# Gated delta net in a two-layer trunk: the decay block's product in front of the state's product, inverse copies of odd pairs on VectorE, and memsets moved ahead

## The chip, the core and the metric

The kernel runs on one core of one Trainium2 chip. The metric is device time in microseconds (us), the median of the runs of one kernel. Before the change it is 2989.25 us over three runs (2982.93 to 2990.8).

## What is computed

A trunk of two layers on a sequence of 1024 positions with 1024 features, all in float32. Layer 0 mixes with a gated delta net of 8 heads, layer 1 with a retention layer of 4 heads; behind each mixer stand a layer norm and a gated convolution feed-forward. The change touches only the delta net. Cut to what matters, with chunks of 64 in the reference:

```python
kk = strict_lower(einsum(kb, k) * decay)
sol = triangular_solve(kk + eye, [v * beta, kb * exp(gc)])
u, w = sol
qk = lower(einsum(q, k) * decay)
def step(state, inp):
    q_n, k_n, u_n, w_n, qk_n, g_n = inp
    v_new = u_n - w_n @ state
    o = (q_n * exp(g_n)) @ state + qk_n @ v_new
    state = state * exp(g_last) + (k_n * exp(g_last - g_n)).T @ v_new
    return state, o
```

Per head, the state of a chunk depends on that of the chunk before it. Everything else of the layer is matrix products that can be put anywhere between.

## The kernel before

**Work.** Here a chunk has 128 positions, so a head has 8 chunks (`NCH`). The delta net is written as Python generators: `gates`, `filler`, `t_path`, `t_decay`, `t_chain`, `prep`, `dt_half`, `scan`, `tail`, `load_q`. The function `run` decides at build time in which order they issue. It keeps a clock that advances by an assumed cost of each TensorE instruction, and always goes on with the ready generator of best priority. A generator that has issued something whose result it needs says how long that will take, by `yield LAT[...]`: only after that many microseconds of planned TensorE work may it go on. `LAT["s1"]`, `["s2"]` and `["s3"]` (1.9, 1.4 and 1.8) are these for the three legs of a scan step, `LAT["T0"]` that for the copies in `t_chain`. Generators also wait for named events (`after_ev`) and for free buffers (`take`, `give`). The order is then fixed on TensorE; every other engine has its instructions in the order in which they were written down, and works them off one after the other.

**The filler.** `filler` has the lowest priority. Its list `items` names projections of 128 features each: "c" (a convolved q, k or v projection that stays in SBUF), "s" (the same, stored to memory and loaded later by a second "c" entry or by `load_q`), "z" (the gate's projection). Each projection is 16 units of three 512-column products, `acc<-hT,wl` and two `acc<-hT,wh`; the units go into the places where nothing of higher priority is ready. Behind each "c" and "s" come a ScalarE copy and scale per half (L485, L488), three VectorE multiply-adds per half (L490) and a SiLU (L491).

**Heads.** Heads go in two groups of four ("quads"), in each quad two pairs: pair 0 and pair 2 are even, 1 and 3 odd. For a quad, `t_decay` makes the decay block of each head (`U`), `t_path` the k-k products and then a forward substitution on VectorE that inverts the four 32x32 diagonal blocks of every chunk; results are `RX` and `TX`. `t_chain` (per pair) copies these into `T0` (L926, three copies of 32x256 per head) and into the inverse's tile `R` (L937 on ScalarE for two row blocks, L939 on GpSimd for the other two, 32x128 each), after zeroing `R` on GpSimd (L931), and then completes the inverse by small products (`mm<-T,U`, `mm<-R,xa` and others). `prep` transposes and scales v and k (evictions L1003, L1012), `dt_half` makes the decay block of q and k, `DT` (L1032).

**The scan step.** `scan` runs per head; the four heads of a quad are in it together. Even pairs write to the PSUM banks named `sc`, odd pairs to those named `mm`, two banks each. In step n all products of a head go to four quarters of one bank: p1 = k times state, p4 = q times state, p2 = `R` times v (named `sc<-qkv,R`), p5 = `U` times w (the state's product, `sc<-w,U`), and p3 = `DT` times w (the decay block's product, `sc<-w,DT`), in the quarter of p1. VectorE makes the new v from p1 (L1059), ScalarE makes w from p2 (L1063) and scales p4 (L1065); VectorE makes the next state `Sn` from p5 (L1073; L1071 in step 0) and adds p3 to the output (L1081). Before the change the state's product and the instruction for `Sn` are issued first, then the decay block's product. All TensorE instructions are issued through helpers, so that they carry line L714 (products) or L717 (transposes); the tile's name tells them apart.

Of the kernel before, what the change touches and what calls it, by code (L numbers as in the profile page):

```python
# [9 lines left out]
F32 = mybir.dt.float32  # L10
# [23 lines left out]
def trunk_kernel(ctx: ExitStack, tc, A):  # L34
# [11 lines left out]
    def tl(tag, shape, dt=F32, name=None):  # L46
        return sb.tile(shape, dt, tag=tag, name=name or tag, bufs=BUFS[tag])

    def two(tag, dt=F32, name=None):
        if tag in ("qkv", "auh"):  # L50
            return tl(tag, [P, HALF], dt, name), tl(tag, [P, HALF], dt, name)
        t = tl(tag, [P, 2, HALF], dt, name)
        return t[:, 0], t[:, 1]
# [659 lines left out]
    def pm(out, lhsT, rhs, start=True, stop=True, cost=0.216):  # L713
        pq(pe.matmul(out, lhsT, rhs, start=start, stop=stop), cost)  # L714
# [4 lines left out]
    def after_ev(*names):  # L719
        return ("ev", names)  # L720

    def emit(name, lat=0.0):
        events[name] = clk[0] + lat
# [45 lines left out]
    def take(tag, n):  # L769
        while free[tag] < n:  # L770
            yield lambda: free[tag] >= n
        free[tag] -= n

    def give(tag, n):
        free[tag] += n
# [39 lines left out]
    dve.tensor_scalar(mneg, m_incl, 1e30, -1e30, ALU.mult, ALU.add)  # L815

    def decay(h):
        for q4 in range(2):
            yield from take("t2", 2)
            gm = [tl("t2", [P, 4, P], F32R, name="gm") for _ in range(2)]  # L820
            for t, g in zip(gm, (gh64, gl64)):
                pool.tensor_tensor(t, bm(m_incl, 4), bc(g[:, q4s(q4), h], P), ALU.mult)
            yield LAT["gm"]
            pt = acc_tile() if h > 3 else sc_tile()
            pm(pt, m_lowr, gm[1], start=True, stop=False)
            pm(pt, m_lowr, gm[0], start=False, stop=True)
            dve.tensor_tensor(U[h][:, q4s(q4)], v4(pt), bm(mneg, 4), ALU.add)
            give("t2", 2)

    def t_decay(p):  # L830
        yield after_ev(("g",), ("DD", p - 1), ("T", p // 2 - 1))
# [10 lines left out]
    def t_path(g):  # L842
        heads = quads[g]
        X = None
        if g:
            yield after_ev(*[("Sh", h) for h in quads[g - 1]])
        for hh, h in enumerate(heads):
            yield after_ev(("f", GH + h), ("DD", h // 2))
            sk = tl("sm", [P, NCH], name="sk")
            cj[h] = tl("sm", [P, NCH], name="cj")  # L850
            ir[h] = tl("sm", [P, NCH], name="ir")
            for q4 in range(2):
                yield LAT["kk"]
                pt = mm_tile()
                for c in range(4):
                    ks = fx(GH + h, q4 * 4 + c)
                    pm(pt[:, c * P:(c + 1) * P], ks, ks)
                for c in range(4):
                    n = q4 * 4 + c
                    junk = tl("S", [P, P], name="jk")  # L860
                    dve.scalar_tensor_tensor(junk, pt[:, c * P:(c + 1) * P], 1.0, ident, ALU.mult, ALU.mult,
                                             accum_out=sk[:, n:n + 1])
                qs = q4s(q4)
                dve.tensor_scalar(sk[:, qs], sk[:, qs], 1e-6, None, ALU.add)
                dve.reciprocal(cj[h][:, qs], sk[:, qs])
                dve.tensor_tensor(cj[h][:, qs], cj[h][:, qs], beta[:, qs, h], ALU.mult)
                if q4:
                    pool.tensor_tensor(ir[h], sk, phalf, ALU.pow)
                for c in range(4):
                    n = q4 * 4 + c  # L870
                    dve.scalar_tensor_tensor(U[h][:, n], pt[:, c * P:(c + 1) * P], cj[h][:, n:n + 1],
                                             U[h][:, n], ALU.mult, ALU.mult)
            if X is None:
                yield from take("lane", 1)
                X = tl("lane", [P, 32, 32], name="X")
            for b in range(4):
                bs = slice(32 * b, 32 * b + 32)
                act.activation(X[bs, :, hh * 8:hh * 8 + 8].rearrange("p i c -> p c i"), U[h][bs, :, bs], AF.Copy)
        yield from take("lane", 2)
        yield LAT["X"]  # L880
        Y = tl("lane", [P, 32, 32], name="Y")
        dve.transpose(flat(Y), flat(X))
        T = tl("lane", [P, 32, 32], name="T")
        pool.memset(T, 0.0)
        pool.memset(flat(T)[:, 0:1024:33], 1.0)
        tmp = tl("fs", [P, 256], name="fs")
        for j in range(31):
            ni, nj = 31 - j, j + 1
            tv = tmp[:, 0:ni * nj].rearrange("p (i j) -> p i j", j=nj)
            dve.tensor_tensor(tv, bc(Y[:, j + 1:, j], nj), bm(T[:, j, 0:nj], ni), ALU.mult)  # L890
            ts_ = T[:, j + 1:, 0:nj]
            dve.tensor_tensor(ts_, ts_, tv, ALU.subtract)
            if j % 3 == 2:
                yield LAT["fs"]
        RX = tl("lane", [P, 32, 32], name="RX")
        dve.transpose(flat(RX), flat(T))
        TP = tl("lane", [P, 32, 32], name="TP")
        act.activation(TP, T.rearrange("p i j -> p j i"), AF.Copy)
        TX = tl("lane", [P, 32, 32], name="TX")
        dve.transpose(flat(TX), flat(TP))  # L900
        RTX[g] = (RX, TX)
        give("lane", 1)
        emit(("T", g), LAT["T"])
# [4 lines left out]
    def dx_(h, n):  # L908
        return DT[h, n // 4][:, n % 4 * P:n % 4 * P + P]

    def t_chain(p):
        heads = pairs[p]
        yield after_ev(("T", p // 2))
        RX, TX = RTX[p // 2]
        cx = p % 2 * 16
        yield from take("auh", 4)
        yield from take("lane", 1)
        T0 = tl("lane", [P, 2, NCH, 64], name="T0")
        lo, hi = slice(0, 64), slice(64, 128)
        for hh, h in enumerate(heads):  # L920
            ch = slice(cx + hh * 8, cx + hh * 8 + 8)
            pool.memset(T0[0:32, hh, :, 32:64], 0.0)
            for b in range(3):
                bs = slice(32 * b, 32 * b + 32)
                cs = slice(32, 64) if b == 1 else slice(0, 32)
                act.activation(T0[bs, hh, :, cs], TX[bs, :, ch].rearrange("p i c -> p c i"), AF.Copy)  # L926
        for hh, h in enumerate(heads):
            R[h] = two("auh", F32, "R")
            for q4 in range(2):
                Rv = v4(R[h][q4])  # L930
                pool.memset(Rv, 0.0)  # L931
                ch = slice(cx + hh * 8 + q4 * 4, cx + hh * 8 + q4 * 4 + 4)
                for b in range(4):
                    bs = slice(32 * b, 32 * b + 32)
                    src = RX[bs, :, ch].rearrange("p i c -> p c i")
                    if b < 2:
                        act.activation(Rv[bs, :, bs], src, AF.Copy)  # L937
                    else:
                        pool.tensor_copy(Rv[bs, :, bs], src)  # L939
        if ("T0", p ^ 1) in events:  # L940
# [98 lines left out]
    def scan(p, h):  # L1039
# [9 lines left out]
        for n in range(NCH):  # L1049
# [14 lines left out]
            if n:  # L1064
                act.activation(vn, p4, AF.Copy, scale=egc[:, n, h:h + 1])  # L1065
            yield LAT["s2"]
            if n < NCH - 1:
                pm(p5, U[h][:, n], w)
                Sn = tl(home, [P, P], name="Sn")
                if n == 0:  # L1070
                    dve.tensor_copy(Sn, p5)  # L1071
                else:
                    dve.scalar_tensor_tensor(Sn, S0, egl[:, n, h:h + 1], p5, ALU.mult, ALU.add)  # L1073
                S0 = Sn
            if n % 4 == 0:
                yield after_ev(("D", h, n // 4))
            pm(p3, dx_(h, n), w)
            if n == 0:
                act.activation(vn, p3, AF.Copy)
            else:  # L1080
# [58 lines left out]
    def filler(items):  # L1139
        for kind, ti in items:  # L1140
# [44 lines left out]
            if kind != "z":  # L1185
# [5 lines left out]
                    emit(("f", ti), LAT["fv"])  # L1191
            bg_step(acc_tile)

    LAT = {"kk": 3.6, "exp": 3.2, "ld": 6.0, "g1": 12.0, "gm": 3.0, "mm": 2.2, "T": 6.0, "X": 3.4, "fs": 4.85, "T0": 5.5, "t1": 2.0, "t2": 3.3, "t3": 1.7, "D": 2.7, "s1": 1.9, "s2": 1.4, "s3": 1.8, "tail": 12.5, "ssq": 9.3, "fv": 4.0}
    events["T", -1] = events["DD", -1] = 0.0
    pairs = [(2 * p, 2 * p + 1) for p in range(GH // 2)]
    c, z = "c", "z"
# [1 line left out]
    s = "s"  # L1199
    quads = [tuple(range(4)), tuple(range(4, 8))]  # L1200
    items = [("h", 1), ("h", 2), ("h", 3), (c, K + 2), (c, K + 3), (z, 0), (c, V), (c, V + 1), (c, V + 2), (c, V + 3), (c, 1),
             (s, 2), (s, 3), (s, K + 4), (s, K + 5), (s, K + 6), (z, 1), (z, 2), (c, K + 4), (c, K + 5), (c, K + 6),
             (c, K + 7), (s, 6), (s, 7), (c, V + 4), (c, V + 5), (c, V + 6), (c, V + 7), (c, 4), (c, 5),
             (z, 3), (z, 4), (z, 5), (z, 6), (z, 7)]
    todo = [(-1.0, gates()), (9.0, filler(items)), (0.3, t_path(0)), (2.3, t_path(1)), (0.9, load_q(1)), (2.9, load_q(3))]
    for p in range(4):
        q = p & 2
# [889 lines left out]
```

## Time and profile before

| what | us |
|---|---|
| median of three runs | 2989.25 |
| the profiled execution's own time | 3002.74 |
| its span in the profile | 3000.6 |
| TensorE (PE) busy | 2835.7 (95%) |
| weight loads (PEld) busy | 2309.8 |
| VectorE (DVE) busy | 2180.1 (73%) |
| ScalarE (ACT) busy | 1310.3 |
| GpSimd (POOL) busy | 505.3 |

The profiled execution's time lies 0.45% above the median. The delta net's generators cover roughly 100 to 698 us of the span. PE is busy nearly everywhere, so time is read as the waits of PE and as the clock that it was granted: the row PEclk of the page and the clock column of the view by windows give that as a share of full speed. A busy time at clock 0.5 holds half the work. An entry "PE sc L714 <- DVE Sn L1073" in the view of waits reads: PE stood idle before a product into a bank `sc` until the VectorE instruction at line 1073 was done. A matmul of 128x128 float32 counts as two instructions in the trace (two passes).

### The profile page before, as it was taken

The numbers are of one execution on the slowest core, as the hardware profiler recorded it, in microseconds if no ns is written. First come the engines' busy times: TensorE is split into PE (matmuls) and PEld (weight loads), VectorE is DVE, ScalarE is ACT, GpSimd is POOL, SyncE is SP. The second block draws the span as 40 slices with busy tenths as digits, with TensorE's granted clock in tenths as the row PEclk, the third lists the DMA queues.
The fourth block names the chain that finished last, engine by engine and source line by source line (L and its number), as shares of the span: only waits on it lengthen the run. The fifth ranks groups of instructions, "written<-read, shape, count | busy, mean of one in ns | idle before, by whom it ended". The sixth has DMA issues, their size and how long they took to land. (4 is left out here: it accounts for less than half of the span.)

```text
span 3000.6 us, 38751 instructions
## 1 busy us (share of the span) xinstructions
PE 2835.7 (95%) x13594; PEld 2309.8 (77%) x13594; DVE 2180.1 (73%) x3846; ACT 1310.3 (44%) x2413; POOL 505.3 (17%) x509
## 2 busy tenths in 40 slices
PE   8998799979999999999999999999999999999997
PEld 6787678867777888887778777777777787888886
DVE  5795559547588888867776775566778787777779
ACT  4754345433454444553543333122335444444543
POOL 0311031100002333210000011422111022332201
PEclk9997999899999999999999999999999999999999
DMA  7222233236425565565543355665564154434853
GB/s 268 96 85 90 86 111 110 68 111 209 162 71 175 187 210 180 197 236 167 176 134 127 109 174 174 213 190 160 179 236 141 73 175 144 136 132 151 305 186 113
DMA packets 253460, 468.44 MB, mean 156 GB/s; under 512 B 24209, under 2 KB 77841, under 8 KB 253265
## 3 DMA queue, kind: packets, MB, share of 16 engines
q1 hardware_dynamic: 218272, 409.59, 41.5%
q10 hardware_dynamic: 32352, 47.72, 4.3%
q0 software_dynamic: 2640, 8.65, 0.8%
q8 instruction: 107, 1.75, 0.2%
q14 instruction: 89, 0.72, 0.1%
HBM read 348.43 MB, written 117.44 MB: 155 GB/s over the span
## 5 line engine op out<-in xcount | busy, mean ns | idle before, releaser
L714 PE MATMUL acc<-hT,wh 128*128 128x512 f32 x960 | 302.2, 396 | 0.0
L1559 PE MATMUL acc<-bb,ab 128*128 128x512 f32 x984 | 236.2, 398 | 13.3 <-DVE bb L90 11.6
L1559 PEld LDWEIGHTS acc<-bb,ab 128*128 128x128 f32 x984 | 186.3, 191 | 57.4 <-DVE bb L90 16.0
L1261 PE MATMUL acc<-T,wb 128*128 128x512 f32 x840 | 203.5, 391 | 8.5 <-DVE wb L90 8.4
L714 PEld LDWEIGHTS acc<-hT,wh 128*128 128x128 f32 x960 | 183.9, 192 | 34.9
L89 ACT ACTIVATE ab<-ar 128x512 fp32r<-128x512 f32 x210 | 130.3, 626 | 173.8 <-PE mm L303 48.8
L714 PE MATMUL acc<-hT,wl 128*128 128x512 f32 x480 | 201.0, 419 | 2.8 <-DVE wl L90 1.6
L411 POOL TENSOR_TENSOR xg<-xg,gb 128x512 f32<-128x512 f32 x48 | 63.5, 1325 | 780.8 <-DMA xg<-xs 476.2
L1261 PEld LDWEIGHTS acc<-T,wb 128*128 128x128 f32 x840 | 156.6, 188 | 45.9 <-DVE wb L90 11.6
L90 DVE TENSOR_TENSOR wl<-wr,wh 128x1024 fp32r<-128x1024 f32 x98 | 123.1, 1256 | 94.6 <-ACT wh L89 94.0
L90 DVE TENSOR_TENSOR ab<-ar,ab 128x512 fp32r<-128x512 f32 x210 | 147.2, 706 | 58.0 <-ACT ab L89 58.0
L1724 POOL TENSOR_TENSOR o<-o 128x512 f32<-128x512 f32 x80 | 137.4, 1727 | 283.6 <-DVE o L1716 138.8
L89 ACT ACTIVATE wh<-wr 128x1024 fp32r<-128x1024 f32 x98 | 103.7, 1059 | 164.6 <-PE acc L714 60.5
L90 DVE TENSOR_TENSOR wb<-wr,wb 128x512 fp32r<-128x512 f32 x162 | 117.9, 732 | 72.4 <-ACT wb L89 70.7
L90 DVE TENSOR_TENSOR wb<-mm,wb 128x512 fp32r<-128x512 f32 x216 | 145.7, 683 | 26.2 <-ACT wb L89 25.3
L89 ACT ACTIVATE wb<-mm 128x512 fp32r<-128x512 f32 x216 | 124.4, 596 | 79.5 <-DVE mm L1315 76.6
L1693 DVE SCALAR_TENSOR_TENSOR o<-g,vc,o 128x512 f32<-128x512 f32 (+2 forms) x176 | 153.8, 892 | 3.8 <-ACT o L1688 3.1
L89 ACT ACTIVATE wb<-wr 128x512 fp32r<-128x512 f32 x162 | 98.3, 627 | 104.8 <-DMA wr<-in_ffn_up 44.3
L1331 ACT ACTIVATE pc<-acc 128x512 f32<-128x512 f32 x143 | 84.7, 592 | 132.9 <-PE acc L1261 83.6
L714 PE MATMUL acc<-wh,hT 128*128 128x512 f32 x384 | 135.1, 415 | 1.0 <-DVE vv L90 1.0
L110 PE MATMUL acc<-T,wb 128*128 128x512 f32 x292 | 115.4, 395 | 5.7 <-DVE wb L90 5.7
L239 DVE SCALAR_TENSOR_TENSOR ada<-mvw,e,ada 128x512 f32<-128x512 f32 x140 | 105.0, 750 | 15.8 <-DMA mvw<-in_ada_w 15.4
(669 smaller groups left out, 7427.8 us busy)
## 6 DMA issues: line engine op xcount, KB each, us to landing
wr<-in_ffn_up SPq DMA_DIRECT2D x92, 512.0 KB, 4.2
mvw<-in_ada_w SPq DMA_DIRECT2D x80, 512.0 KB, 4.6
ad<-o SPq DMA_DIRECT2D x154, 256.0 KB, 3.0
ar<-ad SPq DMA_DIRECT2D x154, 256.0 KB, 3.9
Br<-in_ffn_down SPq DMA_DIRECT2D x88, 256.0 KB, 3.5
wr<-in_ret_wv SPq DMA_DIRECT2D x32, 512.0 KB, 4.1
ar<-od SPq DMA_DIRECT2D x56, 256.0 KB, 5.2
wr<-in_gdn_wqkv SPq DMA_DIRECT2D x24, 512.0 KB, 3.5
```

The source lines that it names most:

```text
L89: act.activation(dst_h, src, AF.Copy)
L90: eng.tensor_tensor(dst_l, src, dst_h, ALU.subtract)
L110: mm(acc, wl[:, k], hl[0], start=first, stop=False)
L239: dve.scalar_tensor_tensor(a, wr[:, kk], e[:, k:k + 1], a, ALU.mult, ALU.add)
L411: pool.tensor_tensor(x, x, gb[0], ALU.mult)
L714: pq(pe.matmul(out, lhsT, rhs, start=start, stop=stop), cost)
L1261: return pe.matmul(*a, skip_group_check=True, **kw)
L1331: act.activation(t, X, AF.Copy)
L1559: return pe.matmul(*args, skip_group_check=True, **kw)
L1693: dve.scalar_tensor_tensor(tv, gv[:, c0 - j:c1 - j], w[:, 2 - j:3 - j], tv, ALU.mult, ALU.add)
L1724: (dve if fp == 0 else pool).tensor_tensor(o[d], o[x], o[y], op)
```

## The change

Five things change, all in the delta net:

- In a scan step the decay block's product (p3) is issued in front of the state's product (p5). The instruction for `Sn` still comes before the addition of p3 on VectorE.
- In `t_chain` of odd pairs the copies into `T0` and the first two row blocks of `R` are written for VectorE in place of ScalarE: per pair 6 copies of 32x256 and 8 of 32x128.
- `t_chain` takes the tiles of `R` and zeroes them when `t_path` reaches the event "X", ahead of the forward substitution, and no longer between the copies.
- `decay` of the heads of the second quad uses buffers of the tag "auh" in place of "t2". The odd scans hold all three "t2" buffers, so these decay blocks stood behind the scans of the first quad; now they can stand within them.
- The table: `LAT["T0"]` goes from 5.5 to 8.0, and in `items` the projection K+6 is no longer stored and loaded again but made once, in its later place, while z3 comes ahead.

```diff
     def decay(h):
+        home = "auh" if h > 3 else "t2"
         for q4 in range(2):
-            yield from take("t2", 2)
-            gm = [tl("t2", [P, 4, P], F32R, name="gm") for _ in range(2)]
+            yield from take(home, 2)
+            gm = [tl(home, [P, 4, P], F32R, name="gm") for _ in range(2)]
...
-            give("t2", 2)
+            give(home, 2)
...
         yield from take("lane", 2)
+        emit(("X", g))
         yield LAT["X"]
...
     def t_chain(p):
         heads = pairs[p]
+        yield after_ev(("X", p // 2))
+        yield from take("auh", 4)
+        for h in heads:
+            R[h] = two("auh", F32, "R")
+            for q4 in range(2):
+                pool.memset(R[h][q4], 0.0)
         yield after_ev(("T", p // 2))
         RX, TX = RTX[p // 2]
         cx = p % 2 * 16
-        yield from take("auh", 4)
         yield from take("lane", 1)
+
+        def block(out, src):
+            if p % 2:
+                dve.tensor_copy(out, src)
+            else:
+                act.activation(out, src, AF.Copy)
...
-                act.activation(T0[bs, hh, :, cs], TX[bs, :, ch].rearrange("p i c -> p c i"), AF.Copy)
+                block(T0[bs, hh, :, cs], TX[bs, :, ch].rearrange("p i c -> p c i"))
...
-                        act.activation(Rv[bs, :, bs], src, AF.Copy)
+                        block(Rv[bs, :, bs], src)
...
             yield LAT["s2"]
+            if n % 4 == 0:
+                yield after_ev(("D", h, n // 4))
+            pm(p3, dx_(h, n), w)
             if n < NCH - 1:
                 pm(p5, U[h][:, n], w)
                 Sn = tl(home, [P, P], name="Sn")
...
-            if n % 4 == 0:
-                yield after_ev(("D", h, n // 4))
-            pm(p3, dx_(h, n), w)
...
-             (s, 2), (s, 3), (s, K + 4), (s, K + 5), (s, K + 6), (z, 1), (z, 2), (c, K + 4), (c, K + 5), (c, K + 6),
+             (s, 2), (s, 3), (s, K + 4), (s, K + 5), (z, 1), (z, 2), (z, 3), (c, K + 4), (c, K + 5), (c, K + 6),
...
-             (z, 3), (z, 4), (z, 5), (z, 6), (z, 7)]
+             (z, 4), (z, 5), (z, 6), (z, 7)]
```

**TensorE, second step of the first quad's scans.** Four heads in one step, two in banks `sc` and two in banks `mm`; the words in brackets are the engines whose semaphores the instruction waits for. Before:

```order
L714 MATMUL sc_2683<-w_2723,U_823 128x128 [waits Activation_49]
L714 MATMUL sc_2683<-w_2723,DT_2136 128x128 [waits DVE_49]
L714 MATMUL sc_2687<-w_2731,U_880 128x128 [waits Activation_49]
L714 MATMUL sc_2687<-w_2731,DT_2136 128x128 [waits DVE_49]
L714 MATMUL mm_2718<-w_2720,U_1005 128x128
L714 MATMUL mm_2718<-w_2720,DT_2139 128x128 [waits DVE_49]
L714 MATMUL mm_2726<-w_2728,U_1093 128x128
L714 MATMUL mm_2726<-w_2728,DT_2139 128x128 [waits DVE_49]
```

The same place with the change:

```order
L714 MATMUL sc_2715<-w_2734,DT_2136 128x128 [waits Activation_49]
L714 MATMUL sc_2715<-w_2734,U_823 128x128
L714 MATMUL sc_2719<-w_2742,DT_2136 128x128 [waits Activation_49]
L714 MATMUL sc_2719<-w_2742,U_880 128x128
L714 MATMUL mm_2729<-w_2731,DT_2139 128x128
L714 MATMUL mm_2729<-w_2731,U_1005 128x128
L714 MATMUL mm_2737<-w_2739,DT_2139 128x128
L714 MATMUL mm_2737<-w_2739,U_1093 128x128
L714 MATMUL acc_2771<-q_2490,qkv_916 128x128 [waits DMAHW5_49]
L714 MATMUL sc_2777<-Sn_2753,qkv_651 128x128 [waits DVE_49]
```

Every product with `DT` waited for VectorE; now it stands first and waits, if at all, for ScalarE, the product with `U` behind it waits for nothing, and the first product of the next step waits for VectorE.

**VectorE, behind the forward substitution of the first quad.** `RX` and `TX` are its transposed results, L1003 (with the change L1014) evicts the transposed v, L490 is the convolution of a filler projection. Before:

```order
L896 STREAM_TRANSPOSE RX<-T 128x1024
L490 SCALAR_TENSOR_TENSOR oq<-raw,vc,oq 128x512
L900 STREAM_TRANSPOSE TX<-TP 128x1024
L1003 TENSOR_TENSOR qkv<-acc,ir 128x512
L490 SCALAR_TENSOR_TENSOR oq<-raw,vc,oq 128x512
L1003 TENSOR_TENSOR qkv<-acc,ir 128x512 x3
L511 TENSOR_SCALAR ssq_2148<-ssq_2148 128x8
```

With the change:

```order
L898 STREAM_TRANSPOSE RX<-T 128x1024
L490 SCALAR_TENSOR_TENSOR oq<-raw,vc,oq 128x512
L902 STREAM_TRANSPOSE TX<-TP 128x1024
L928 COPY R<-RX 32x4x32 x8
L1014 TENSOR_TENSOR qkv<-acc,ir 128x512
L490 SCALAR_TENSOR_TENSOR oq<-raw,vc,oq 128x512
L928 COPY T_2111<-TX 32x8x32 x6
L1014 TENSOR_TENSOR qkv<-acc,ir 128x512 x2
L511 TENSOR_SCALAR ssq_2148<-ssq_2148 128x8
```

Eight copies now stand in front of the first eviction of v and six more in front of the second.

**ScalarE at the same place.** `sq` (L509) are squares for a norm, four from each of two PSUM banks, `xa` belongs to the small products. Before:

```order
L898 ACTIVATE TP<-T 128x1024
L937 ACTIVATE R<-RX 32x4x32 x16
L509 ACTIVATE sq,ssq_2148<-acc 128x128 x3
L926 ACTIVATE T_2070<-TX 32x8x32 x6
L491 ACTIVATE oq<-oq 128x512
L926 ACTIVATE T_2103<-TX 32x8x32 x6
L509 ACTIVATE sq,ssq_2148<-acc 128x128 x4
```

With the change:

```order
L900 ACTIVATE TP<-T 128x1024
L930 ACTIVATE R<-RX 32x4x32 x8
L509 ACTIVATE sq,ssq_2148<-acc 128x128 x7
L930 ACTIVATE T_2086<-TX 32x8x32 x6
L509 ACTIVATE sq,ssq_2148<-acc 128x128
L491 ACTIVATE oq<-oq 128x512
```

The fourth square, which empties the first of the two banks, stood behind 28 copies and now stands behind 8.

More of the change, by code (lines that the diff above doesn't have):

```diff
@@ L925, in t_chain @@
                 cs = slice(32, 64) if b == 1 else slice(0, 32)
-                act.activation(T0[bs, hh, :, cs], TX[bs, :, ch].rearrange("p i c -> p c i"), AF.Copy)
+                block(T0[bs, hh, :, cs], TX[bs, :, ch].rearrange("p i c -> p c i"))
         for hh, h in enumerate(heads):
-            R[h] = two("auh", F32, "R")
             for q4 in range(2):
                 Rv = v4(R[h][q4])
-                pool.memset(Rv, 0.0)
                 ch = slice(cx + hh * 8 + q4 * 4, cx + hh * 8 + q4 * 4 + 4)
@@ L1192, in filler @@
             bg_step(acc_tile)
-    LAT = {"kk": 3.6, "exp": 3.2, "ld": 6.0, "g1": 12.0, "gm": 3.0, "mm": 2.2, "T": 6.0, "X": 3.4, "fs": 4.85, "T0": 5.5, "t1": 2.0, "t2": 3.3, "t3": 1.7, "D": 2.7, "s1": 1.9, "s2": 1.4, "s3": 1.8, "tail": 12.5, "ssq": 9.3, "fv": 4.0}
+    LAT = {"kk": 3.6, "exp": 3.2, "ld": 6.0, "g1": 12.0, "gm": 3.0, "mm": 2.2, "T": 6.0, "X": 3.4, "fs": 4.85, "T0": 8.0, "t1": 2.0, "t2": 3.3, "t3": 1.7, "D": 2.7, "s1": 1.9, "s2": 1.4, "s3": 1.8, "tail": 12.5, "ssq": 9.3, "fv": 4.0}
     events["T", -1] = events["DD", -1] = 0.0
```

## The prediction

> **What bounds the kernel now.** The page comes first: PE is busy for 95% of the span, and its clock is 0.9 or better in 40 coarse slices. Next come windows cut at the stages of the delta net, because an average over 3000 us hides them. The columns are the stretch, its length, busy time and count of each engine, granted clock, DMA share and GB/s.
>
> ```profile
> PE 2835.7 (95%) x13594; PEld 2309.8 (77%) x13594; DVE 2180.1 (73%) x3846; ACT 1310.3 (44%) x2413; POOL 505.3 (17%) x509
> 100.00:234.00 134.00, 128.14 (x608) 105.86 (x607) 111.06 (x284) 80.12 (x164) 28.03 (x37) 1.00 0.31 99
> 234.00:298.00 64.00, 50.95 (x613) 45.35 (x613) 31.57 (x62) 29.21 (x63) 8.40 (x24) 0.76 0.24 78
> 298.00:400.00 102.00, 82.56 (x477) 70.46 (x476) 49.68 (x125) 35.96 (x96) 12.29 (x16) 0.93 0.26 86
> 400.00:536.00 136.00, 130.43 (x621) 108.37 (x620) 111.43 (x285) 75.92 (x162) 30.53 (x41) 0.99 0.34 111
> 536.00:594.00 58.00, 56.35 (x651) 49.81 (x649) 26.83 (x55) 29.39 (x69) 7.71 (x20) 0.85 0.21 72
> 594.00:698.00 104.00, 80.26 (x482) 68.50 (x482) 52.48 (x137) 37.19 (x94) 8.41 (x8) 0.93 0.32 108
> ```
>
> The two scans (298 to 400, 594 to 698) leave PE idle for 19.4 and 23.7 us and run at clock 0.93; the stages of the forward substitution (100 to 234, 400 to 536) are nearly full. At 234 to 298, the inverse's chain of the first quad, there is a hole of 13 us and a clock of 0.76. VectorE has 50 of 102 us in a scan, so no engine is full there: what ends PE's idle time must be a wait. The waits of PE, first scan and then second, name it (total us, times, longest):
>
> ```profile
> PE sc L714 <- DVE Sn L1073: 9.2, 12, 1.8
> PE mm L714 <- DVE Sn L1073: 5.8, 10, 1.0
> PE sc L714 <- DVE qkv L1059: 2.9, 1, 2.9
> PE mm L714 <- DVE Sn L1071: 0.8, 2, 0.4
> PE sc L714 <- DVE Sn L1071: 0.8, 2, 0.4
> ...
> PE mm L714 <- DVE Sn L1073: 12.1, 12, 4.8
> PE sc L714 <- DVE Sn L1073: 6.5, 12, 1.3
> PE acc L717 <- DVE qkv L1101: 2.2, 2, 1.9
> PE mm L714 <- ACT qkv L1065: 1.4, 2, 1.3
> PE mm L714 <- DVE Sn L1071: 0.8, 2, 0.4
> PE sc L714 <- DVE Sn L1071: 0.8, 2, 0.4
> ```
>
> Almost all of it is one wait: for `Sn`, 16.6 us in the first scan and 20.2 in the second, 54 times. The timeline of one such place (start, length, engine, instruction, count, idle time before it) shows which product stands there.
>
> ```profile
> 602.03 0.30 PEld L714 LDWEIGHTS sc<-w,U 128*128 128x128 f32 x2
> 602.14 0.39 PE L714 MATMUL sc<-w,U 128*128 128x128 f32 x2
> 602.57 0.35 DVE L1073 SCALAR_TENSOR_TENSOR Sn<-Sn,eg,sc 128x128 f32<-128x128 f32 x1
> 602.97 0.30 PEld L714 LDWEIGHTS sc<-w,DT 128*128 128x128 f32 x2 [0.63 <-DVE Sn L1073]
> 602.97 0.49 PE L714 MATMUL sc<-w,DT 128*128 128x128 f32 x2 [0.44 <-DVE Sn L1073]
> 603.18 0.30 PEld L714 LDWEIGHTS sc<-w,U 128*128 128x128 f32 x2
> ```
>
> The product with `DT` does not read `Sn`. It waits because VectorE reads the state's product out of the same bank. The next product's weights are loaded 0.21 us behind its own (603.18 against 602.97), so without the wait it would have started 0.21 us after 602.14; it started 0.83 us after. That is 0.62 us lost, where the waits show 0.44: the end of a pipelined product is modelled late by about 0.18 us.
>
> **The scans: the wait that goes.** The first term is 36.8 us of waits for `Sn` plus 54 times 0.18, which is 9.7: **46 us** of TensorE time. With the decay block's product first, no read of the bank stands between the two products. It needs only w, as the state's product did before it. What is late next is the first product of the following step, which needs `Sn`; `Sn` itself comes 0.21 us later, since its product is second. From the start of the state's product to the end of `Sn` the rows above give 0.78 us, and the planner leaves 1.8 us of other work there, so the plain round trip is covered, by the other heads' products and filler units.
>
> **The scans: waits that come.** Bounds: nothing, if the planned times always suffice, and 46 us and more, if every wait moves to the next product. Of the 36.8 us, 54 times 0.44 are the plain round trip, 23.8; the other 13 are places where VectorE was late because of work ahead in its queue (longest 4.8 us). That lateness stays; I let half of it, 6 us, come back in front of products that read `Sn` or v. The product with `DT` now takes the wait for w on ScalarE. One step shows its size:
>
> ```profile
> 600.36 0.60 PE L714 MATMUL sc<-qkv,R 128*128 128x128 f32 x4
> 600.78 0.37 ACT L1063 ACTIVATE w<-sc,cj 128x128 f32<-128x128 f32 x1 [4.44 <-PE sc L714]
> 601.04 0.36 ACT L1065 ACTIVATE qkv<-sc,eg 128x128 f32<-128x128 f32 x1
> 601.29 0.37 ACT L1063 ACTIVATE w<-sc,cj 128x128 f32<-128x128 f32 x1
> ```
>
> w is done 0.79 us after its product starts, 1.30 with a second head's in front; the planner leaves 1.4 behind the product, so it fits narrowly: 4 us for the times when it doesn't. Together **10 us come back**, the value between the bounds that lies near the lower one, because the single row of a product waiting for anything but `Sn` in mid-scan is the one of 2.9 us.
>
> **The clock.** The scans hold 82.6 and 80.3 us busy at 0.93, which full speed would do in 5.8 and 5.6 us less. The stage from 100 to 234 us, 96% busy, has 1.00. Bounds 0 and 11; I take three quarters, as three quarters of the waits go: **8 us**.
>
> The clock of pieces of the first scan speaks for that: 0.83 and 0.91, where the waits' longest single entries were 1.8 and 2.9 us.
>
> ```profile
> 320.00:340.00 20.00, 16.11 (x85) 14.01 (x85) 10.94 (x31) 5.24 (x13) 3.26 (x5) 0.83 0.19 66
> 340.00:360.00 20.00, 15.78 (x93) 13.52 (x92) 12.51 (x33) 8.56 (x29) 3.44 (x4) 0.91 0.17 52
> ```
>
> The Trainium skill, "TensorE: Matmul & The Clock Gate" (section "HAM oscillation — how this bites in real kernels"), says that what costs the clock is a gap of more than about 3.4 us. By that rule short waits would cost no clock, this term would be 0, and the sum 8 us smaller. The rows disagree: the clock was low with no gap that long in the first scan.
>
> **The inverse's chain.** At 240 to 256 us TensorE waits for a bank that ScalarE empties:
>
> ```profile
> 236.49 2.58 ACT L937 ACTIVATE R<-RX 32x128 f32<-32x128 f32 x6 [0.33 <-DVE RX L896]
> 238.16 0.65 DVE L1003 TENSOR_TENSOR qkv<-acc,ir 128x512 f32<-128x512 f32 x1
> 238.87 0.33 PE L717 MATMUL acc<-cst,qkv 128*128 128x128 f32 x1 [2.21 <-DVE qkv L1003]
> ...
> 253.14 1.11 PE L717 MATMUL acc<-cst,qkv 128*128 128x128 f32 x4 [10.05 <-ACT sq L509]
> ...
> L926 ACT ACTIVATE T<-TX 32x256 f32<-32x256 f32 x12 | 7.5, 627 | 0.1
> L937 ACT ACTIVATE R<-RX 32x128 f32<-32x128 f32 x16 | 6.8, 425 | 0.5 <-DVE RX L896 0.3
> ```
>
> The fourth square stood behind 16 copies of 0.425 and 12 of 0.627. Now it stands behind 8 of the former: from 236.49 that is 239.9, and with four squares about 241. But 14 copies go to VectorE, in front of evictions of v. This trace has no copy from SBUF to SBUF on VectorE; the nearest rows are of the same shapes out of PSUM:
>
> ```profile
> L971 DVE TENSOR_SCALAR R<-mm 32x128 f32<-32x128 f32 x32 | 7.8, 279 | 0.3
> L967 DVE TENSOR_SCALAR T<-mm 32x256 f32<-32x256 f32 x8 | 3.3, 418 | 5.4 <-PE mm L714 5.3
> L490 DVE SCALAR_TENSOR_TENSOR qkv<-raw,vc,qkv 128x512 f32<-128x512 f32 x87 | 69.9, 803 | 17.4 <-ACT qkv L488 13.9 <-POOL gm L822 2.7 <-POOL ir L868 0.2
> ```
>
> 8 times 0.28 and 6 times 0.42 are 4.8 us, and the next evictions end about 246 in place of 242. TensorE goes on at about 246 to 247 where it went on at 253.1: **6 us gained** (bounds 0 and 11). In the second quad there was no hole (1.65 us idle in the whole chain), and the same copies now delay evictions that were on time: **4 us lost** (bounds 0 and 7). Net 2 us. The memsets are GpSimd's, whose 505 us leave room; they cost nothing.
>
> **The gap between the scans.** The second quad's decay blocks move into the first scan, on GpSimd and TensorE, the same number of instructions. K+6 and more convolutions fall into 400 to 536: by the new list 9 to 10 where there were 7, each six L490, 4.8 us of VectorE; some 12 us more on an engine with 25 us idle there. The stage at 100 to 234 has nine convolutions, and its PE idles no more than that at 400 (6 against 6 us). I charge **3 us**, bounds 0 and 12. The store and reload of K+6 go, hidden DMA either way.
>
> **The end of the second scan.** Two waits there, 2.2 and 1.4 us, come from a planner with nothing left to issue. With the change 12 filler units (three products each) stand behind and between the last steps: **3 us** gained.
>
> **Sum.** −46 + 10 − 8 − 2 − 3 + 3 = −46 us. Against the profiled execution's own 3002.7 that is 2957; it lies 13.5 us above the median, so against the median of 2989 the forecast is **2943 us**. Its own range, with waits that come between 0 and 25, the clock between 11 and 0 and the chain as bounded, is 2920 to 2965.
>
> **Rivals.** *Half of the wait comes back.* The scan legs are planned so tightly that without the accidental pauses VectorE and ScalarE are late by a few tenths at each of some 160 dependent products. For it: 13 us of lateness now. Against: no such wait but one in mid-scan. 23 us in place of 10 come back, and the clock gives 4 in place of 8: −29, **2960**; worse, with 35, 2972.
>
> *VectorE takes back the chain.* Its copies and GpSimd's copies (0.41 us each by the row below) keep each other out: 14 waits of 0.41 per quad, 11.5 us in all, behind which stand the evictions. Against it: the eviction and the convolution beside GpSimd's run (238.16, 0.65; the mean of L490 is 0.80) are not lengthened. **2955**, and 2964 with the whole 12 of the gap.
>
> ```profile
> L939 POOL COPY R<-RX 32x128 f32<-32x128 f32 x32 | 13.4, 418 | 1.5
> ```
>
> The Trainium skill, "SBUF — State Buffer" (section "Who interferes with whom"), names this: VectorE in a two-port mode and GpSimd lock each other out for whole instructions. By that rule the copies would cost what this rival says; no run here shows such a copy yet.
>
> *Slower: the recurrence is the bound.* If less than 1.04 us (0.83 + 0.21) of other work stands between the two products of a head and its next step's first, the whole wait moves there, and each is 0.21 us longer because `Sn` starts later: 54 times 0.21, 11 us, less 2 for the other terms: **2999**. Against it: three other heads' products and 1.8 us planned.
>
> *It does not do what it says*: the second product waits for something at the bank as the first did, and only the small terms remain: **2987**. The order shows no such wait.
>
> **How the numbers follow.** Forecast 0.60, half back 0.18, VectorE 0.09, no change 0.07, slower 0.06. A measurement of this kernel tells about 0.3% from no change, 9 us, so faster means under 2980: the first three, 0.87. The range takes in the forecast's bounds and the first two rivals, 2915 to 2975, and leaves out the last two.
>
> **What would show it.** Right: no wait "`DT` for `Sn`" in the waits; scans of some 80 us; clock near 1.00 in them; the 10 us wait for `sq` gone. Wrong: waits for `Sn` of like sum in front of `sc<-Sn,qkv`, waits for w above 10 us, or PE holes over 8 us at both chains.

## The result and the profile after

The changed kernel takes 2918.7 us (median of four runs, 2916.51 to 2920.75) against 2990.03 (four runs, 2982.93 to 2991.6): a ratio of 0.9766, with a 95% interval of 0.9748 to 0.9783, or 71 us less. Run again later beside other kernels it took 2919.27. The forecast was 46 us less: the sign and the main step were right, the size was 25 us too small.

The profiled execution after took 2919.49 us, 0.8 above its median; that of before took 3002.74, 12.7 above its own. So the two traces differ by 83 us where the kernels differ by 71, and some 10 us of the traces' difference lie where the change does next to nothing (4.5 ahead of the delta net's `RX`, 5.3 behind its end). First the page's row of engines and the windows of the changed kernel, cut at the same stages as in the prediction (stretch, length, busy time and count of PE, PEld, DVE, ACT and POOL, granted clock, DMA share, GB/s):

```profile
PE 2799.6 (96%) x13594; PEld 2288.3 (78%) x13594; DVE 2183.0 (75%) x3874; ACT 1299.3 (45%) x2387; POOL 494.8 (17%) x509
100.00:229.50 129.50, 123.66 (x589) 102.20 (x588) 106.77 (x280) 76.04 (x160) 24.34 (x35) 1.00 0.31 99
229.50:288.00 58.50, 52.15 (x620) 46.04 (x619) 37.93 (x76) 21.86 (x49) 8.68 (x23) 0.82 0.26 86
288.00:358.00 70.00, 68.71 (x470) 61.77 (x470) 46.49 (x125) 35.83 (x95) 21.44 (x20) 1.00 0.36 117
358.00:477.00 119.00, 117.18 (x565) 97.67 (x564) 100.35 (x274) 71.08 (x141) 20.39 (x38) 1.00 0.37 120
477.00:538.00 61.00, 54.11 (x654) 47.60 (x653) 39.10 (x81) 27.81 (x78) 9.39 (x21) 0.89 0.16 53
538.00:611.00 73.00, 71.61 (x485) 64.51 (x484) 46.95 (x130) 33.35 (x86) 7.43 (x7) 1.00 0.40 137
```

The scans (288 to 358, 538 to 611) took 206 us before and take 143. PE's idle time in them fell from 43.2 us to 2.7, and the clock rose from 0.93 to 1.00. PE's busy time fell by 22.5 us, though these windows hold about the same work: 959 instructions before and 955 now, of them 251 and 260 products of filler units. So the 22.5 us are the clock and the late modelled ends, and nearly all of the 63 us are gained in the scans. The stage from 358 to 477 stands for the earlier 400 to 536; it is 17 us shorter because its records hold 38 filler products fewer (455 in place of 493, some 15 us), which now stand in the second scan and behind it.

These are all waits of PE left in the first scan, and behind the dots the one in the second (total us, times, longest):

```profile
PE sc L714 <- DVE qkv L1092: 0.8, 1, 0.8
PE sc L714 <- DVE qkv L1070: 0.3, 1, 0.3
PE mm L714 <- DVE qkv L1070: 0.2, 1, 0.2
...
PE mm L714 <- DVE qkv L1092: 1.4, 1, 1.4
```

No product waits for `Sn` any longer; of the 36.8 us, 2.7 of another kind are there in its place. The timeline of one step of the two heads in the banks `sc` shows why (start, length, engine, instruction, count, idle time before it; lines of other tiles left out):

```profile
311.15 0.39 PE L714 MATMUL sc<-w,DT 128*128 128x128 f32 x2
311.38 0.39 PE L714 MATMUL sc<-w,U 128*128 128x128 f32 x2
311.87 0.35 DVE L1087 SCALAR_TENSOR_TENSOR Sn<-Sn,eg,sc 128x128 f32<-128x128 f32 x1 [2.00 <-PE sc L714]
312.74 0.38 PE L714 MATMUL sc<-w,DT 128*128 128x128 f32 x2
312.96 0.39 PE L714 MATMUL sc<-w,U 128*128 128x128 f32 x2
313.44 0.35 DVE L1087 SCALAR_TENSOR_TENSOR Sn<-Sn,eg,sc 128x128 f32<-128x128 f32 x1 [1.03 <-PE sc L714]
313.88 0.61 PE L714 MATMUL sc<-Sn,qkv 128*128 128x128 f32 x4
315.22 0.61 PE L714 MATMUL sc<-Sn,qkv 128*128 128x128 f32 x4
```

A head's two products with w start 0.22 to 0.23 us apart, where they were 0.83 apart. By the order of issue, the first head's state is made from 311.87 to 312.22 and first read at 313.88; the second's is made from 313.44 to 313.79 and first read at 315.22. So 2.50 and 2.26 us lie between a state's product and its first reader, where the round trip takes 0.84, and in them stand the other heads' products and filler units. The round trip is as long as before; it now lies beside work that does not need it.

At the inverse's chains, and in the gap between the scans, the longest waits of PE are these (first chain, second chain, gap):

```profile
PE acc L717 <- ACT sq L509: 4.4, 1, 4.4
PE acc L714 <- ACT sq L509: 1.1, 1, 1.1
...
PE acc L717 <- DVE qkv L1014: 5.5, 1, 5.5
PE mm L714 <- ACT xb L992: 0.7, 1, 0.7
...
PE mm L714 <- DVE U L872: 1.4, 1, 1.4
PE acc L714 <- DVE wl L90: 0.5, 1, 0.5
```

The hole of the first chain fell from 13.1 us of idle time to 6.4; the second chain's idle time rose from 1.6 us to 6.9; the gap's fell from 5.6 to 1.8.

### The profile page after: what moved, and what is told of

It reads as the page before. It is cut to its first block, busy times and chain, and to the rows that moved or that the text cites. A ratio compares the mean times of both kernels' runs of the same rounds, so it can differ in the third digit from the quotient of the medians.

```text
span 2917.7 us, 38768 instructions
## 1 busy us (share of the span) xinstructions
PE 2799.6 (96%) x13594; PEld 2288.3 (78%) x13594; DVE 2183.0 (75%) x3874; ACT 1299.3 (45%) x2387; POOL 494.8 (17%) x509
## 4 chain that ended last, share of the span: by engine, by line
PE 68%; DVE 16%; DMA 8%; ACT 4%; issue 3%; POOL 1%; SPq 0%; ACTq 0%; DVEq 0%; POOLq 0%
PE acc L714 14%; PE acc L1272 8%; PE acc L110 5%; PE acc L111 5%; PE acc L112 5%; PE sc L1272 4%; PE acc L1570 4%; PE sc L714 4%; PE mm L714 3%; PE sc L110 2%; DVE o L1704 2%; PE sc L111 2%; PE sc L112 2%; DMA mvw<-in_ada_w 2%; DVE wb L90 2%
## 5 line engine op out<-in xcount | busy, mean ns | idle before, releaser
L1735 POOL TENSOR_TENSOR o<-o 128x512 f32<-128x512 f32 x80 | 125.5, 1578 | 285.2 <-PE acc L112 185.2
```

The source lines that it names most:

```text
L1735: (dve if fp == 0 else pool).tensor_tensor(o[d], o[x], o[y], op)
```

## The experiments

The theory: TensorE stood at the product with `DT` because VectorE was reading the same PSUM bank. The swap takes that read from between the two products, and planned work hides the round trip where it goes instead. The rivals on record: part of the wait comes back; the gain is VectorE's copies or the list; the recurrence decides. Times stand beside runs of the kernel before on the same chip.

### The parts one by one

**The swap alone**, in the kernel before:

```diff
             yield LAT["s2"]
+            if n % 4 == 0:
+                yield after_ev(("D", h, n // 4))
+            pm(p3, dx_(h, n), w)
             if n < NCH - 1:
...
-            if n % 4 == 0:
-                yield after_ev(("D", h, n // 4))
-            pm(p3, dx_(h, n), w)
```

> The kernel before with nothing changed but the order of the two products in a scan step (decay block's product first). Theory of the bank wait: all 54 waits of the DT product for Sn go (46 us), the clock in the scans returns to 1.00 (8 to 11 us), few waits come: 2990 - 52 = 2938, scans of about 80 us each, the 10 us wait for sq and the clock of 0.76 at the chain stay. Rival, that the gain comes from the other edits (item list, decay blocks inside the first scan, copies) and the swap only moves the wait to the next product that reads Sn: 2975 or more, with waits for Sn in front of sc<-Sn,qkv.

Measured: 2933.24 against 2990.84, ratio 0.9804 (0.9781 to 0.9827), 58 us less. The two scans, in the kernel before and then with the swap, in windows that hold the same products but for three (from 1 us ahead of the first w to 1 us behind the last):

```profile
296.00:404.30 108.30, 88.86 (x509) 75.78 (x508) 53.13 (x131) 37.42 (x100) 14.91 (x20) 0.94 0.25 83
591.60:692.60 101.00, 79.44 (x470) 67.65 (x469) 49.31 (x129) 34.95 (x90) 6.43 (x6) 0.93 0.28 97
...
295.40:376.30 80.90, 77.56 (x507) 69.55 (x506) 49.80 (x130) 36.92 (x100) 14.65 (x19) 0.98 0.34 111
560.90:631.80 70.90, 68.04 (x471) 61.47 (x470) 47.30 (x129) 34.99 (x90) 6.88 (x6) 1.00 0.40 138
```

The same work takes 151.8 us in place of 209.3, so the whole 58 us are gained in the scans: 34.8 of them are idle time of PE (41.0 to 6.2), 22.7 its busy time. No wait for `Sn` is left. The 10.1 us at the first chain are still there.

**Everything but the swap**, in the changed kernel:

```diff
-            if n % 4 == 0:
-                yield after_ev(("D", h, n // 4))
-            pm(p3, dx_(h, n), w)
             if n < NCH - 1:
...
+            if n % 4 == 0:
+                yield after_ev(("D", h, n // 4))
+            pm(p3, dx_(h, n), w)
```

> The changed kernel with the state's product first again. Theory of the bank wait: the waits of the DT product for Sn are back, 35 to 40 us shown, clock below 0.95 in the scans: 2919 + 52 = 2971, which leaves about 19 us for all other edits. Rival, that the other edits carry the gain: below 2940.

Measured: 2975.09, ratio 0.9938 (0.9914 to 0.9962), 16 us less. Its waits of PE:

```profile
PE mm L714 <- DVE Sn L1084: 18.2, 24, 3.3
PE sc L714 <- DVE Sn L1084: 11.2, 24, 0.8
PE acc L717 <- DVE qkv L1014: 5.5, 1, 5.5
PE acc L717 <- ACT sq L509: 4.5, 1, 4.5
...
PE mm L714 <- DVE Sn L1082: 1.5, 4, 0.4
...
PE sc L714 <- DVE Sn L1082: 1.2, 3, 0.4
```

All the waits for `Sn` are back, 32.1 us of them, while the chains look as in the changed kernel. The clock of the scans, which I expected below 0.95, fell less: 0.98 in the first (285.4 to 376.3) and 0.95 in the second (554.4 to 654.9). In these windows the scans take 191.4 us, and 144.1 for the same products in the changed kernel. The two effects are apart, and they add up: 58 and 16 are 74 where the whole change gives 71.

### Is it the bank?

**An own bank for the decay block's product**, in the kernel before, with its order kept:

```diff
                 yield after_ev(("D", h, n // 4))
+            p3 = acc_tile()[:, 0:P]
             pm(p3, dx_(h, n), w)
```

> The kernel before with its order kept (state's product first), but the decay block's product goes to a bank of its own, taken from the acc banks. If the wait is for the read of the bank by VectorE, it goes without any change of order: like the swap alone, about 2940 to 2950 (some waits for acc banks may come, since VectorE empties them behind Sn). Rival, that the DT product waits for Sn for another reason (order on VectorE, data): as before, 2990, with the same 37 us of waits.

Measured: 2929.36, ratio 0.9799 (0.9773 to 0.9826), 61 us less, as much as the swap and more than I expected. The product still stands behind the instruction for `Sn` in the program, and only its bank is another. Of the waits for `Sn` one is left, and the scans are full at full clock (a line of its waits, then its windows):

```profile
PE mm L714 <- DVE Sn L1073: 1.2, 1, 1.2
```

```profile
293.00:370.00 77.00, 74.90 (x499) 67.04 (x498) 49.82 (x129) 36.27 (x99) 14.43 (x20) 1.00 0.35 117
555.00:626.00 71.00, 67.86 (x474) 61.38 (x473) 48.34 (x134) 36.19 (x93) 7.11 (x7) 1.00 0.44 145
```

So the wait was for the shared bank, and not for VectorE's result. It is a semaphore of the program (`waits DVE` in the order of TensorE's instructions, ahead of the prediction); what the chip would do without it, no run here shows.

**Both together**: the own bank in the changed kernel, with `DT` first and with `U` first (the line `p3 = acc_tile()[:, 0:P]` ahead of the product, and for the second the order of before).

> The changed kernel, in its order, with the decay block's product in a bank of the acc set. My theory: the scans wait for nothing any more, so nothing is left to gain there: 2919, between 2912 and 2924. Rival, that a bank shared by both products still costs something (the next step's product waits for the addition): 2905 or less.

> The changed kernel with the state's product first and the decay block's product in a bank of the acc set, so that the next state starts 0.2 us earlier and nothing waits for the bank. My theory: scans full as in the changed kernel, 2919, between 2910 and 2924, since the planned work hides the round trip either way. Rival, that the recurrence's length counts: 56 times 0.21 or 12 us less, 2907.

Measured: 2923.17, ratio 0.9772 (0.9748 to 0.9797), and 2921.88, ratio 0.9766 (0.9741 to 0.979). Neither can be told from the changed kernel or from the other. With the state's product first, `Sn` starts earlier; that gains nothing, so the recurrence does not set the time.

### What hides the round trip

**No planned time for the third leg**, in the changed kernel:

```diff
-"s3": 1.8,
+"s3": 0.0,
```

> The changed kernel with the planner's time behind the state's product set to 0 in place of 1.8. My theory, that the planned work between the state's product and the next step's first product hides the new round trip: waits for Sn come back in front of sc<-Sn,qkv and mm<-Sn,qkv, up to 0.6 us each at 56 places, 20 to 35 us in all, and the clock in the scans falls: 2940 to 2965. Rival, that the engines keep up anyway and the plan plays no part: within 10 us of 2919.

Measured: 2978.36, ratio 0.9956 (0.9939 to 0.9973), 60 us slower than the changed kernel and more than I expected. The view of the products that read `Sn`: idle time of PE ahead of them (us, times):

```profile
  DVE qkv L1092: 40.8, 45
  ACT qkv L1090: 8.0, 8
  DVE Sn L1087: 2.1, 2
```

50.9 us, 0.93 at a time, now stand at the first product of the next step. The planner put no filler between, and the whole gain of the swap is gone. Nearly all waits end with L1092, the addition behind `Sn`, or with L1090, which stands for it in step 0: the last read of a bank which, with two banks of a name and two heads, the same head's next step writes again. The clock in its scans was 0.96 and 0.95:

```profile
288.00:368.00 80.00, 57.40 (x369) 50.21 (x367) 38.71 (x103) 25.34 (x70) 14.80 (x14) 0.96 0.12 40
566.00:660.00 94.00, 68.27 (x432) 59.54 (x432) 44.81 (x119) 27.24 (x83) 6.28 (x6) 0.95 0.22 76
```

### The copies on VectorE

**All copies on ScalarE**, as before the change:

```diff
-            if p % 2:
+            if p < 0:
                 dve.tensor_copy(out, src)
```

> The changed kernel with the odd pairs' copies back on ScalarE. My theory: the first quad's chain gets its wait of about 10 us for sq back and the second quad's loses its 5.5 us wait for the eviction; net 2919 + 1 to 4 = about 2921. Rival, that the copies on VectorE are a main part of the gain outside the swap: 2930 or more.

Measured: 2930.08 against 2993.71, ratio 0.9783 (0.976 to 0.9807). The median lies at the rival's 2930 and not at my 2921, but the five runs spread from 2922 to 2935 and the interval overlaps that of the changed kernel, so the times do not decide between the two. Its waits of PE at the two chains:

```profile
PE acc L717 <- ACT sq L509: 10.1, 1, 10.1
PE acc L717 <- ACT qkv L491: 7.9, 1, 7.9
```

With the rest of the change the second chain has a hole of its own on ScalarE, 7.9 us, which the kernel before did not have. The copies on VectorE take 6 us off the first and 2 off the second.

**On VectorE in the first quad only**, since I charged the second with a loss:

```diff
-            if p % 2:
+            if p == 1:
```

> The changed kernel with the odd pair's copies on VectorE in the first quad only and on ScalarE in the second. My theory: the 5.5 us wait of the second quad's chain goes and the first quad keeps its 4.4 in place of 10: 2919 - 4 = about 2915. Rival, that in the second quad ScalarE's 28 copies now hold up the start of the chain by as much: 2919 to 2925.

Measured: 2922.66, ratio 0.9765 (0.9745 to 0.9785): no difference. My theory fell here; the trace has a wait of 7.8 us in place of the 5.5:

```profile
PE acc L717 <- ACT qkv L491: 7.8, 1, 7.8
PE acc L717 <- ACT sq L509: 4.5, 1, 4.5
```

**GpSimd's copies on ScalarE**, to see VectorE's without them beside it (a single run, no interval):

```diff
                     else:
-                        pool.tensor_copy(Rv[bs, :, bs], src)
+                        act.activation(Rv[bs, :, bs], src, AF.Copy)
```

> The changed kernel with GpSimd's copies into R on ScalarE, so that nothing runs on GpSimd while VectorE copies. Read for the durations only. If VectorE's copies and GpSimd's keep each other out, the copies of 32x128 take about 0.28 us in place of 0.43 and those of 32x256 about 0.35 to 0.42 in place of 0.49. Rival, that such a copy takes that long by itself: 0.43 and 0.49 again. The time gets worse, since ScalarE has 16 copies more per quad: the wait for sq about 8 us or more.

Measured: 2934.11, longer than the changed kernel. What counts are the durations of VectorE's copies (least, median, longest in ns; first and last start), here and then in the changed kernel:

```profile
L928 DVE COPY R<-RX x16: 211/274/316, 237.9 to 490.5; 32x128 f32<-32x128 f32 x16
L928 DVE COPY T<-TX x12: 364/371/378, 241.4 to 493.3; 32x256 f32<-32x256 f32 x12
```

```profile
L928 DVE COPY R<-RX x16: 394/430/458, 233.6 to 483.9; 32x128 f32<-32x128 f32 x16
L928 DVE COPY T<-TX x12: 381/482/591, 238.4 to 487.5; 32x256 f32<-32x256 f32 x12
```

The same copy takes 0.274 us alone and 0.430 beside GpSimd's copies. The changed kernel's timeline, at three moments of the first chain, shows how:

```profile
233.53 0.39 POOL L950 COPY R<-RX 32x128 f32<-32x128 f32 x1
233.64 0.39 DVE L928 COPY R<-RX 32x128 f32<-32x128 f32 x1
...
234.41 0.38 POOL L950 COPY R<-RX 32x128 f32<-32x128 f32 x1
234.49 0.43 DVE L928 COPY R<-RX 32x128 f32<-32x128 f32 x1
...
235.28 0.39 POOL L950 COPY R<-RX 32x128 f32<-32x128 f32 x1
235.36 0.43 DVE L928 COPY R<-RX 32x128 f32<-32x128 f32 x1
```

The two engines go in step, with each VectorE copy 0.08 to 0.11 us behind one of GpSimd's. Only VectorE pays: GpSimd's first 15 copies last 7.14 us there and 7.08 in the kernel before. (In the second quad they last 8.10 and 7.48, but those beside VectorE's copies of 32x128 take 0.40 to 0.43 us, before 0.40 to 0.42.)

### The buffers, the list, and the change once more

**The second quad's decay blocks in "t2"** (`home = "t2"` for all heads), and **the old list** (`items` as before the change), each in the changed kernel; and the changed kernel itself once more.

> The changed kernel with the second quad's decay blocks back in the t2 buffers, behind the first quad's scans. Theory of the bank wait: the place of these blocks is worth little, 2919 to 2928. Rival, that it is these blocks inside the scan that filled TensorE: 2940 or more.

> The changed kernel with the old list of projections (K+6 stored and loaded again, z3 late). Of the 16 us that the edits besides the swap are worth, the copies gave about 5 and the decay blocks' place about 3; if the rest is the list, 2919 + 5 to 10 = 2924 to 2929. Rival, that the list is worth nothing: 2919.

> The changed kernel itself, on the same chip as the three others, so that differences of a few us between them can be read: 2919.

Measured: 2922.0, ratio 0.9773 (0.9749 to 0.9797), for the buffers: at most some 3 us, which can't be told from nothing. For the list 2927.19, ratio 0.9781 (0.9756 to 0.9806), beside 2919.27, ratio 0.9757 (0.9732 to 0.9782), for the changed kernel on the same chip: 8 us between medians with overlapping intervals. The list is probably worth something; how much stays open. No variant is faster than the changed kernel.

## Why the forecast was right, and too small

**The wait that goes (46): right.** All 54 waits for `Sn` went; they are back without the swap, and with an own bank one of 1.2 us is left. The late modelled ends and the clock were 9.7 and 8 us in the sum, 17.7 together; with the swap alone PE's busy time for the same work in the scans fell by 22.7, so the two were 5 us too small.

**The waits that come (10): the step that failed in the main term.** "That lateness stays; I let half of it, 6 us, come back", and 4 for w. In the changed scans 2.7 us of waits stand in all, none of them for w; with the swap alone the waits other than for `Sn` rose from 4.3 to 6.0. The lateness of VectorE was real, but it was seen because a product stood directly behind it in a shared bank. The product that now depends on it comes later: the planner leaves 1.8 us, and the two places shown have 2.26 and 2.50 where the round trip takes 0.84. So a lateness of more than 1 us is hidden there; with the 1.8 set to 0, 50.9 us show. The swap was worth 58 us alone, and 56 on top of the rest (2975.09 less 2918.7), where the sum gave 44. Of the 13 us between, some 8 are waits that didn't come and 5 the clock and the ends.

**The clock (8): it rose, but the waits alone do not set it.** I took three quarters of 11; the scans came to 1.00, and to 0.98 and 1.00 with the swap alone. The clock can't be separated from the modelled ends by the busy time, which holds both. Nor does it follow the waits: the kernel before had 36.8 us of waits for `Sn` and 0.93, the kernel without the swap 32.1 us and 0.98 and 0.95, the one without planned time 50.9 us and 0.96 and 0.95. Each is one profiled execution, so how much clock these waits cost stays open. The Trainium skill, "TensorE: Matmul & The Clock Gate" (section "HAM oscillation — how this bites in real kernels"), lets only gaps of more than about 3.4 us cost clock; the first scan of before had 0.93 with no wait above 2.9 us, so the measurement decides against the rule here.

**The chain (2): right net, and the pieces were near.** 7 us gained at the first against 6, 5 lost at the second against 4. Two of its numbers failed. The copies took 0.43 and 0.48 us and not 0.28 and 0.42, so 6.3 us a quad in place of 4.8. And the loss at the second quad was charged against a chain without a hole, but with the rest of the change ScalarE would leave a hole of 7.9 us there. The copies are thus worth 8 us of waits, not 2; the times of that run leave their worth open.

**The gap (3 lost) and the end (3 gained): the gap's sign was wrong.** Its idle time fell by 4 us. The new list and places made no engine late; VectorE had room for the extra convolutions (100 of 119 us busy). The second scan ends with its waits covered, as forecast. All that is not the swap was worth 16 us by its own run (11 to 26 by its interval), where I had 2; it is the sum that is resolved, not its split over list, copies and buffers, and most of these 14 us have no cause shown.

So of the 25 us that the forecast lacked, some 12 are the swap's and some 14 the rest's, less 1 or 2 because the parts overlap.

**The range.** My bounds gave 2920 to 2965, and 2918.7 lies just under that. The range on record starts at 2915, and no term of the sum gives its lower end, so in that much it was luck. At the other end the bounds come out higher than I wrote: with 25 us of waits back, no clock and the chain at its worst they give 2975.

**The rivals.** Half of the wait coming back and the recurrence as the bound did not occur, and the run without planned time shows their condition: they would have held if the planner left no work there. In that run the whole wait moved, as the slower rival has it: 50.9 us of waits, and 2978.36 us, where the kernel without the swap takes 2975.09. VectorE's copies and GpSimd's do slow each other, as the second rival said, but by 0.16 us a copy (0.430 less 0.274) and not by 0.41.

## What to carry to other kernels

When a product waits for a result that it does not read, look at which bank it writes: here the program made it wait for a read of another part of the same bank. Issue all products into a bank ahead of its first reader, or give the odd one a bank of its own; both were worth 58 to 61 us here. Then ask where the reader's round trip goes instead, and how much planned work stands there: if that is more than the round trip with its usual lateness, as the 2.26 us here were, charge little for it.

## What was unexpected in the hardware

A VectorE copy of 32x128 float32 from SBUF to SBUF took 0.274 us alone and 0.430 beside GpSimd's copies of the same shape; one of 32x256 took 0.371 and 0.482. The Trainium skill, "SBUF — State Buffer" (section "Who interferes with whom"), has GpSimd and VectorE in its two-port modes block each other for whole instructions; the trace agrees in that each VectorE copy ends 0.11 to 0.13 us behind GpSimd's, but a pair took 0.44 us, less than 0.274 and 0.39 added, and GpSimd was not slowed. Waits for `Sn` of 0.7 us in the mean, 54 times, went with a clock of 0.93 in the kernel before; with the waits gone, by the swap or by the bank, it was 0.98 to 1.00. But 55 such waits of 0.6 us went with 0.98 and 0.95 in the kernel without the swap, so the waits do not settle the clock by themselves.
